# Windowed attention scored for two heads by 64 tokens and 320 keys at a time

## The chip, the cores and the metric

The kernel runs on one core of a Trainium2 chip. The core has a matrix engine (TensorE, PE in the profile; its weight loads are listed as PEld), VectorE (DVE), ScalarE (ACT), GpSimd (POOL), and SyncE (SP), which issues most of the DMA transfers. The metric is the device time of one execution in microseconds (us), and the smaller one is better.

## The reference

One encoder layer is applied to two groups of 2048 tokens of width 1024 (prompt and sample), which share their weights. Two groups of attention heads read one projection of the normalised input; their gated outputs are joined, projected and added to the input, and a gated embedding is added at the end. The change lies in head group A: 8 query heads of 64 elements, 2 key heads, each serving 4 query heads, and a window of 128 tokens to either side, with a learned sink per head in the denominator.

```python
def windowed_gqa_sink(q, k, v, sink):          # A_BLOCK = WINDOW = 128
    span = A_BLOCK + 2 * WINDOW                # 384 keys for 128 queries
    band = np.abs(si - WINDOW - qi) <= WINDOW
    def block(j):
        sc = jnp.einsum('bqkgd,bskd->bkgqs', qb, kb).astype(jnp.float32) * scale
        sc = jnp.where(valid, sc, -jnp.inf)
        m = jnp.maximum(jnp.max(sc, axis=-1, keepdims=True), sink_f)
        e = jnp.exp(sc - m)
        denom = jnp.sum(e, axis=-1, keepdims=True) + jnp.exp(sink_f - m)
        pr = (e / denom).astype(vb.dtype)
        o = jnp.einsum('bkgqs,bskd->bqkgd', pr, vb)
        return o.reshape(b, A_BLOCK, A_WIDTH)
...
o_a = windowed_gqa_sink(q_a, k_a, v_a, sink_a) * jax.nn.silu(g_a)
```

Of the 384 keys that a block of 128 queries may see, a run of 64 queries sees 320: its own 64 and 128 on either side.

## The kernel before, in words

The kernel has three stages. The first (32 blocks of 128 tokens, numbered f; 16 per sequence, t within it) projects the input for head group A and does its windowed attention. The second does the same for head group B, the neighbourhood attention. The third multiplies the joined outputs with the output and gate weights. Products are made in three parts of a number's high and low half, so that a score product has the high and low half of the keys stacked on the 128 rows of TensorE's array (`ks_a`), and a value product has the high and low half of a value side by side in its 128 columns (`vv`).

TensorE's order is written out by hand: every product (`mm`, line 259) and transpose (`tr`, line 262) is chained to the one before. The main loop draws projection products of the blocks ahead from a stream ("filler": 24 products of 256 columns named `pk`, and 48 of 512 columns named `pq` and `pg`, for each block), and between them puts the steps of attention. A block has two units, one for each key head (`unit_a`, line 652). The list `PLAN_A` (line 88) says at which fraction of a unit's share of filler each step comes; an entry with 1 is a step of this unit, one with 0 a step of the unit before. The other engines mostly follow in order of their readiness.

The steps of one unit before the change, for an interior block (three key blocks of 128):

- `sc` 0 to 3: for each of the unit's four query heads, two products of 384 columns (128 queries by 384 keys; queries' high and low parts) in a PSUM tile, then on DVE one pass that adds the mask and takes the row maximum (`softmax`, line 272). Behind the fourth, `exps` (line 282) makes the exponentials and their sums on ACT.
- `rest`: the second part of the queries' split into high and low halves, which `prep` starts for the next block (`prep_a`, line 641: four transposes `pqt`).
- `den`: the sink is added to the sums, the reciprocal taken, and the gate multiplied by it on POOL.
- `pt` 0 to 2: for each key block, four transposes (one per head) of the exponentials into one PSUM tile, copied out by ACT (high part, line 678) and subtracted by DVE (low part, line 679) into one of three `p_t` buffers.
- `po` 0 to 2: for each key block, two products of 512 columns (four heads by 128 queries) with the values, all three blocks adding up in one PSUM bank.
- `fin`: two transposes of the gate (`pgt`), the sum of high and low value columns, the gating, and the transfer to memory.

At a sequence's first and last block (t = 0 and t = 15) there are two key blocks, so 256 columns of scores, eight transposes and four value products.

Of the kernel before, what the change touches and what calls it, by code (L numbers as in the profile page):

```python
# [11 lines left out]
F32 = mybir.dt.float32  # L12
# [41 lines left out]
def bias_offsets():  # L54
# [31 lines left out]
CP = 2  # L86
KB = 23
PLAN_A = (
    (0.04, 1, "sc", 0), (0.10, 1, "sc", 1), (0.12, 1, "sc", 2), (0.12, 1, "rest", 0), (0.14, 1, "sc", 3),
    (0.14, 1, "rest", 1), (0.14, 0, "po", 0),  # L90
    (0.22, 0, "po", 1), (0.34, 0, "po", 2), (0.36, 1, "den", 0), (0.45, 0, "fin", 0), (0.46, 1, "prep", 0),
    (0.75, 1, "pt", 0), (0.79, 1, "pt", 1), (0.88, 1, "pt", 2),
)
PLAN_B = (
# [6 lines left out]
def emit(ctx, tc, io):  # L101
# [167 lines left out]
                mm(ps, xr[:, a, k, :], w(k, b), k == 0 and i == 0, k == KT - 1 and i == 2)  # L269
                yield cost, k == KT - 1 and i == 2  # L270

    def softmax(i, ps, n, bias, sm):

        s = main.tile([128, 512], F32, tag="s", name="s", bufs=SB)
        nc.vector.tensor_tensor_reduce(out=s[:, :n], in0=ps[:, :n], in1=bias, scale=1.0, scalar=-3.0e38,  # L275
                                       op0=ALU.add, op1=ALU.max, accum_out=sm["mx"][:, i:i + 1])
        sm["s"].append(s)

    def sm_tiles():
        return {"s": [], **{k: ap.tile([128, 4], F32, tag=k, name=k, bufs=3) for k in ("mx", "nm", "den", "rd")}}  # L280

    def exps(sm, n, fct, gs, sink=None):

        mx, nm, den, rd, ss = (sm[k] for k in ("mx", "nm", "den", "rd", "s"))
        if sink is None:
            nc.vector.tensor_scalar_mul(nm, mx, -1.0)  # L286
            yield
        else:
            nc.vector.scalar_tensor_tensor(out=nm, in0=mx, scalar=-1.0, in1=sink[1], op0=ALU.mult, op1=ALU.min)
        for n_, i in enumerate((0, 2, 1, 3) if sink is None else range(4)):  # L290
            ex = nc.scalar.activation(ss[i][:, :n], ss[i][:, :n], AF.Exp, bias=nm[:, i:i + 1],  # L291
                                      accum_out=den[:, i:i + 1])
            if sink is None and n_ == 0:
                P(ex)
        if sink is not None:
            es = ap.tile([128, 4], F32, tag="es", name="es", bufs=3)
            nc.vector.tensor_tensor(out=es, in0=sink[0], in1=nm, op=ALU.add)
            nc.scalar.activation(es, es, AF.Exp)
            yield
            nc.vector.tensor_tensor(out=den, in0=den, in1=es, op=ALU.add)  # L300
        nc.vector.reciprocal(out=rd, in_=den)
        nc.vector.tensor_scalar_mul(rd, rd, fct)
        g2 = ap.tile([128, 4, HD], F32, tag="g2", name="g2", bufs=2)
        nc.gpsimd.tensor_tensor(out=g2, in0=gs.rearrange("p (h d) -> p h d", h=4),
                                in1=rd.unsqueeze(2).broadcast_to([128, 4, HD]), op=ALU.mult)
        sm["g2"] = g2.rearrange("p h d -> p (h d)")
        yield
# [129 lines left out]
    sums = [dram.tile([4, 128, 4, 512], F32, tag=f"sums{i}", name=f"sums{i}") for i in range(2)]  # L437
    w_gate_c = copied(io["w_gate"], DM, 1024)
    snk = ap.tile([128, 2, 8], F32, tag="snk", name="snk")
    nc.sync.dma_start(snk[:, 0, :], io["sink"].partition_broadcast(128))  # L440
    nc.vector.tensor_scalar_mul(snk[:, 1, :], snk[:, 0, :], -1.0)
    tab = [ap.tile([128, 2, NT, 16], F32, tag="vp", name=f"tab{i}", bufs=3) for i in range(2)]
    for i in range(4):
# [3 lines left out]
        raws_g += load_first(main.tile([128, 2, 512], F32, tag="p_t", name="ws", bufs=3), j, 768, 512)  # L447
    for j in range(4, KT):
        raws_g += load_first(ap.tile([128, 1, 512], F32, tag="qg", name="wg", bufs=6), j, 768, 512)
    mask = ap.tile([128, 384], F32, tag="vp", name="mask", bufs=3)  # L450
    nc.sync.dma_start(mask, io["band"])
    load_next()
    load_next()
# [187 lines left out]
    def prep_a(f):  # L641
        q = held[f][0]
        pqt = ptile([128, 512], "ms", "pqt")
        for i in range(4):
            tr(pqt[:, 128 * i:128 * i + 128], q[:, 2 * i:2 * i + 2, :].rearrange("p h d -> p (h d)"))
        q1 = [ap.tile([128, 512], F32R, tag="q1", name="q1", bufs=3) for _ in range(2)]
        q2 = [q2s[f % 2][:, e] for e in range(2)]
        drain(split_q(pqt, q1, q2, 0))
        qrest[f] = split_q(pqt, q1, q2, 1)
        return q1, q2  # L650

    def unit_a(f, kv):
        s, t = divmod(f, NT)
        _, gs, y = held[f]
        k0, k1 = max(0, t - 1), min(NT, t + 2)
        n = 128 * (k1 - k0)
        m0 = 128 * (k0 - t + 1)
        sm, prs, got = sm_tiles(), [], {}

        def sc(i):  # L660
            ps = ptile([128, 512], "sc", "sc")
            for j, q in enumerate(qs[f]):
                mm(ps[:, :n], q[kv][:, 128 * i:128 * i + 128], ks_a[:, kv, 128 * k0:128 * k1], j == 0, j == 1)
            softmax(i, ps, n, mask[:, m0:m0 + n], sm)
            if i == 3:
                got["ex"] = exps(sm, n, y[:, 11:12], gs[:, 256 * kv:256 * kv + 256],
                                 (snk[:, 0, 4 * kv:4 * kv + 4], snk[:, 1, 4 * kv:4 * kv + 4]))
                next(got["ex"])

        def pt(j):  # L670
            if j >= k1 - k0:
                return
            pt = ptile([128, 4, 128], "pt", "pt")
            for i in range(4):
                tr(pt[:, i, :], sm["s"][i][:, 128 * j:128 * j + 128])
            pr = main.tile([128, 2, 512], F32R, tag="p_t", name="pr", bufs=3)
            pf = pt.rearrange("p h q -> p (h q)")
            nc.scalar.copy(pr[:, 0], pf)
            nc.vector.tensor_tensor(out=pr[:, 1], in0=pf, in1=pr[:, 0].bitcast(F32), op=ALU.subtract)
            prs.append(pr)  # L680

        def po(j):
            if j == 0:
                got["po"] = ptile([128, 512], "ms", "po")
            if j < k1 - k0:
                v = vv[:, k0 + j, kv].rearrange("p a d -> p (a d)")
                for i in range(2):
                    mm(got["po"], v, prs[j][:, i], j == 0 and i == 0, k0 + j == k1 - 1 and i == 1)

        def fin(_):  # L690
            pgt = ptile([128, 2, 128], "sc", "pgt")
# [3 lines left out]
            ph2 = got["po"].rearrange("p (i e q) -> p e i q", e=2, q=128)  # L695
            for e in range(2):
                a, z = 64 * e, 64 - 64 * e
                nc.scalar.copy(ot[a:a + 64], ph2[z:z + 64, e])
            for e in range(2):
                a = 64 * e  # L700
                nc.vector.tensor_tensor(out=ot[a:a + 64], in0=ph2[a:a + 64, e], in1=ot[a:a + 64], op=ALU.add)
            nc.vector.tensor_tensor(out=ot, in0=pgt, in1=ot, op=ALU.mult)
# [105 lines left out]
    def unit_b(f):  # L808
# [25 lines left out]
        def sc(h):  # L834
            ps = ptile([128, 512], "sc", "scb")
            for j, q in enumerate(qs[f]):
                mm(ps[:, :n].rearrange("p (r c) -> p r c", c=ncol), q[h % 2][:, 128 * (h // 2):128 * (h // 2) + 128],
                   ks_b[h % 2][:, r0:r0 + nr, h // 2, c0:c0 + ncol], j == 0, j == 1)
            softmax(h, ps, n, bias[:, h, :n], sm)
            if h == 3:  # L840
                got["ex"] = exps(sm, n, hr_b[:, st:st + 1], gs)
                next(got["ex"])

        def pt(x):
# [82 lines left out]
    def ple_ahead(n, tail=False):  # L927

        load_p(n + 1)
        for m in range(KT):  # L930
            ps = ptile([128, TW], "pj", "pple")
            if m == 5 and n + 1 < len(tiles):
                split_p(n + 1)
            flush("p0")
            for k in range(2):
                w, c = early["p"][2 * (m // 4) + k], 128 * (m % 4)
                for i, (a, b) in enumerate(((0, 0), (0, 1), (1, 0))):
                    mm(ps, w[:, a, c:c + 128], p_rs[n][:, k, b], k == 0 and i == 0, k == 1 and i == 2)
                    yield 215
            if tail:  # L940
                ev = main.tile([128, TW], F32, tag="s", name="ev", bufs=SB)
            else:
                ev = ap.tile([128, TW], F32, tag=("ev", "sq")[m // 2 % 2], name="ev", bufs=2)
            P(nc.scalar.copy(ev, ps))
            nc.sync.dma_start(ple_d[n][:, m], ev)

# [315 lines left out]


def _band():
    q = np.arange(128)[:, None]
    k = np.arange(384)[None, :]
    return np.where((k >= q) & (k <= q + 256), 0.0, NEG).astype(np.float32)


# [68 lines left out]
```

## Time and profile before

| what | value |
|---|---|
| median of three runs | 2495.81 us (2495.41 to 2498.2) |
| the profiled execution, its time | 2493.45 us |
| its span in the profile | 2491.5 us |
| granted TensorE clock | 1.0 |
| busy: PE, PEld, DVE, ACT, POOL | 99%, 84%, 70%, 57%, 32% |
| first stage's attention, about | 42 to 774 us of the span |

The span runs from the first to the last instruction of the profiled execution; its time also holds what lies around it. PE counts as busy while any product is in its pipeline, and successive products overlap, so that a product's listed length is longer than its share of PE; the distance between the starts of successive products is that share. A row of a group names the line of code, engine, operation, output and inputs, shapes and count, then busy time, the mean length of one in ns, and the engine's idle time before it with what ended that.

### The profile page before, as it was taken

What the parts mean: (1) busy time and instruction counts of PE and PEld (TensorE: products, weight loads), DVE (VectorE), ACT (ScalarE), POOL (GpSimd) and SP (SyncE); (2) the same over time, 40 slices, a digit from 0 to 9 for tenths busy, and PEclk for the clock granted to TensorE, in tenths of its full rate; (3) what the DMA queues carried; (4) which work ended last, traced back from release to release, by engine and by line L of the source; (5) the groups of instructions that cost most, each with busy time, mean ns of one, the idle gap of its engine ahead of it and who ended that gap; (6) DMA issues with size and microseconds to landing.
All of it is one profiled execution on the core that took longest, in us unless ns stands there. A gap on an engine that the chain in (4) does not pass through costs nothing.

```text
span 2491.5 us, 39866 instructions
## 1 busy us (share of the span) xinstructions
PE 2470.3 (99%) x12920; PEld 2084.8 (84%) x12920; DVE 1733.7 (70%) x4274; ACT 1417.0 (57%) x3341; POOL 786.7 (32%) x1033
## 2 busy tenths in 40 slices
PE   9999999999999999999999999999999999999999
PEld 7888888888888888888888888888788888888887
DVE  7777777777775666666666676776547655687776
ACT  6677766767664566665566666665664222344443
POOL 4444444444434444444444443443110000000000
PEclk9999999999999999999999999999999999999999
DMA  6432233222254466556855566666977455756765
GB/s 207 140 111 97 82 94 100 90 92 94 90 183 139 145 196 183 166 181 189 272 184 182 184 208 197 199 204 217 302 245 279 155 172 176 265 172 219 243 226 169
DMA packets 246656, 438.86 MB, mean 176 GB/s; under 512 B 31920, under 2 KB 86320, under 8 KB 241200
## 3 DMA queue, kind: packets, MB, share of 16 engines
q1 hardware_dynamic: 246160, 436.30, 54.3%
q8 instruction: 103, 1.69, 0.3%
q14 instruction: 105, 0.86, 0.1%
q10 hardware_dynamic: 288, 0.01, 0.0%
HBM read 308.28 MB, written 133.19 MB: 177 GB/s over the span
## 4 chain that ended last, share of the span: by engine, by line
PE 93%; DMA 3%; DVE 2%; ACT 1%; issue 1%; POOL 0%; SPq 0%; DVEq 0%; ACTq 0%; POOLq 0%
PE pvg L260 14%; PE pqk L260 14%; PE acca L1161 13%; PE accc L1161 10%; PE pg L260 7%; PE pq L260 7%; PE scb L260 3%; PE ptb L263 3%; PE sc L260 3%; PE po L260 3%; PE pob L260 3%; PE pk L260 3%; PE pt L263 3%; PE pple L260 3%; DMA p<-p_t 1%; DMA stn<-x_n 1%
## 5 line engine op out<-in xcount | busy, mean ns | idle before, releaser
L291 ACT ACTIVATE s<-s,nm 128x384 f32<-128x384 f32 (+4 forms) x512 | 307.2, 601 | 328.4 <-DVE nm L286 199.5
L260 PE MATMUL pvg<-wb,xr 128*128 128x512 f32 x1536 | 461.4, 407 | 0.0
L260 PE MATMUL pqk<-wa,xr 128*128 128x512 f32 x1536 | 442.3, 410 | 0.0
L260 PEld LDWEIGHTS pqk<-wa,xr 128*128 128x128 f32 x1536 | 266.3, 189 | 37.0
L260 PEld LDWEIGHTS pvg<-wb,xr 128*128 128x128 f32 x1536 | 266.9, 189 | 31.7 <-DVE wb L157 0.8
L356 POOL TENSOR_TENSOR xr<-stx,xr 128x512 fp32r<-128x512 f32 x188 | 241.5, 1294 | 162.5 <-ACT xr L355 154.8
L1143 ACT CAST opd<-raw 128x512 fp32r<-128x512 f32 x224 | 131.5, 618 | 268.4 <-PE acca L1161 115.6
L1144 DVE TENSOR_TENSOR opd<-raw,opd 128x512 fp32r<-128x512 f32 x224 | 146.5, 686 | 143.8 <-ACT opd L1143 143.8
L260 PE MATMUL pg<-wb,xr 128*128 128x512 f32 x768 | 231.5, 409 | 1.0 <-DVE vv L506 1.0
L260 PE MATMUL pq<-wa,xr 128*128 128x512 f32 x768 | 220.5, 400 | 1.4 <-DVE wa L157 1.1
L275 DVE CUSTOM_DVE_ANT_0 s<-scb,bias 128x288 f32<-128x288 f32 (+3 forms) x256 | 141.8, 555 | 103.9 <-PE scb L260 99.0
L142 POOL TENSOR_TENSOR yb<-vrb,power 128x8 f32<-128x8 f32 x64 | 105.3, 1645 | 252.5 <-DVE vrb L747 244.2
L1161 PE MATMUL accc<-opd,wb 128*128 128x512 f32 x768 | 176.7, 389 | 0.0
L1161 PE MATMUL acca<-opd,wa 128*128 128x512 f32 x768 | 175.5, 389 | 0.0
L1161 PE MATMUL acca<-opd,s 128*128 128x512 f32 x768 | 175.4, 389 | 0.0
L1161 PEld LDWEIGHTS acca<-opd,wa 128*128 128x128 f32 x768 | 144.1, 188 | 29.9
L1161 PEld LDWEIGHTS acca<-opd,s 128*128 128x128 f32 x768 | 144.2, 188 | 29.9
L1161 PEld LDWEIGHTS accc<-opd,wb 128*128 128x128 f32 x768 | 144.1, 188 | 29.9
L873 DVE TENSOR_TENSOR otb<-pob,otb 64x512 f32<-64x512 f32 x128 | 88.2, 689 | 112.8 <-ACT otb L872 111.7
L260 PEld LDWEIGHTS pq<-wa,xr 128*128 128x128 f32 x768 | 139.2, 188 | 24.8 <-DVE wa L157 1.9
L260 PEld LDWEIGHTS pg<-wb,xr 128*128 128x128 f32 x768 | 137.1, 189 | 21.9 <-DVE vv L506 1.5
L260 PEld LDWEIGHTS pob<-p_t,vw 128*128 128x128 f32 (+2 forms) x832 | 132.0, 189 | 25.3 <-DVE p_t L854 5.3
(159 smaller groups left out, 5117.8 us busy)
## 6 DMA issues: line engine op xcount, KB each, us to landing
stx<-x_b SPq DMA_DIRECT2D x128, 256.0 KB
vw<-v_d SPq DMA_DIRECT2D x112, 256.0 KB
stx<-x_a SPq DMA_DIRECT2D x64, 256.0 KB
stn<-x_n SPq DMA_DIRECT2D x64, 256.0 KB
v_d<-vb SPq DMA_DIRECT2D x64, 256.0 KB
ple_d<-ev SPq DMA_DIRECT2D x64, 256.0 KB
xres<-x_r SPq DMA_DIRECT2D x64, 256.0 KB
x_d<-r SPq DMA_DIRECT2D x64, 256.0 KB
```

What stands on the lines that cost most here:

```text
L142: nc.gpsimd.tensor_tensor(out=y, in0=v, in1=power.broadcast_to([128, n]), op=ALU.pow)
L260: pinned(nc.tensor.matmul(out, lhsT, rhs, start=start, stop=stop))
L263: pinned(nc.tensor.transpose(out, in_, eye))
L275: nc.vector.tensor_tensor_reduce(out=s[:, :n], in0=ps[:, :n], in1=bias, scale=1.0, scalar=-3.0e38, op0=ALU.add, op1=ALU.max, accum_out=sm[ ...
L291: ex = nc.scalar.activation(ss[i][:, :n], ss[i][:, :n], AF.Exp, bias=nm[:, i:i + 1], accum_out=den[:, i:i + 1])
L356: low.tensor_tensor(out=lo, in0=raw, in1=hi.bitcast(F32), op=ALU.subtract)
L873: nc.vector.tensor_tensor(out=ot[a:a + 64], in0=pq[a:a + 64], in1=ot[a:a + 64], op=ALU.add)
L1143: P(nc.scalar.copy(hi, v))
L1144: P(nc.vector.tensor_tensor(out=lo, in0=v, in1=hi.bitcast(F32), op=ALU.subtract))
L1161: pinned(nc.tensor.matmul(ps, w[k][:, a, c:c + 128], o[:, b], start=i in (0, 1, 4) and k == 0 and j == 0, stop=k == 3 and j == 2, skip_gro ...
```

## The change

The two axes "head" and "half of the queries" are exchanged. A score product now takes two heads by 64 queries instead of one head by 128 queries, so that its 128 rows share one run of 64 tokens, and covers 320 keys instead of 384. `prep_a` writes the transposed queries in that order. The scores of the two halves of a pair of heads lie side by side in one tile of 640 columns (`s2`; three buffers).

The transposes are regrouped by keys. Step `pt` 1 takes the whole key block before for the first half and the whole key block after for the second; `pt` 2 takes the middle block for both. What is left is 64 keys for each half (the lower half of the block after for the first half, the upper half of the block before for the second); these lie next to one another in the tile, and `pt` 0 transposes them together, two transposes of 128 columns, to a tile of 256 columns. In the value products (`part`) of that tile, the first half uses rows 0 to 63 with the lower half of one value block, and the second half uses rows 64 to 127 with the upper half of another. The product on the upper rows is put in the third `po` step and is made to wait for the last score reduction of the next unit, which is behind the product on the lower rows.

The sink has to be added with heads and halves exchanged back, which takes four small additions instead of one; the sink's values are spread by two small copies at the start. At a sequence's end a piece of the score tile is cleared by POOL. In the plan, `po` 0 moves ahead of the fourth scores, `po` 1 from 0.22 to 0.26, `po` 2 from 0.34 to 0.37.

```diff
 PLAN_A = (
-    (0.04, 1, "sc", 0), (0.10, 1, "sc", 1), (0.12, 1, "sc", 2), (0.12, 1, "rest", 0), (0.14, 1, "sc", 3),
-    (0.14, 1, "rest", 1), (0.14, 0, "po", 0),
-    (0.22, 0, "po", 1), (0.34, 0, "po", 2), (0.36, 1, "den", 0), (0.45, 0, "fin", 0), (0.46, 1, "prep", 0),
+    (0.04, 1, "sc", 0), (0.10, 1, "sc", 1), (0.12, 1, "sc", 2), (0.12, 1, "rest", 0), (0.14, 0, "po", 0), (0.14, 1, "sc", 3),
+    (0.14, 1, "rest", 1),
+    (0.26, 0, "po", 1), (0.36, 1, "den", 0), (0.37, 0, "po", 2), (0.45, 0, "fin", 0), (0.46, 1, "prep", 0),
...
     def exps(sm, fct, gs, sink=None):
...
-            nc.vector.tensor_tensor(out=den, in0=den, in1=es, op=ALU.add)
+            for half in range(2):
+                for e in range(2):
+                    rows = slice(64 * e, 64 * e + 64)
+                    nc.vector.tensor_tensor(out=rd[64 * half:64 * half + 64, e::2], in0=den[rows, half::2],
+                                            in1=es[rows, half::2], op=ALU.add)
+            den = rd
...
+    for e in range(2):
+        rows = slice(64 * e, 64 * e + 64)
+        nc.vector.tensor_copy(snk[rows, 0].rearrange("p (a b) -> p a b", b=2),
+                              snk_all[rows, e::2].unsqueeze(2).broadcast_to([64, 4, 2]))
...
-    mask = ap.tile([128, 384], F32, tag="vp", name="mask", bufs=3)
+    mask = ap.tile([128, 320], F32, tag="vp", name="mask", bufs=3)
...
+        halves = pqt.rearrange("p (r x e q) -> p r e x q", r=2, x=2, e=2)
         for i in range(4):
-            tr(pqt[:, 128 * i:128 * i + 128], q[:, 2 * i:2 * i + 2, :].rearrange("p h d -> p (h d)"))
+            tr(halves[:, i // 2, i % 2], q[:, 2 * i:2 * i + 2, :].rearrange("p h d -> p (h d)"),
+               ident.rearrange("p (x q) -> p x q", x=2))
...
+        left, right = t > 0, t < NT - 1
+        span = [(0 if left else 128 - 64 * half, 320 if right else 256 - 64 * half) for half in range(2)]
...
         def sc(i):
+            pair, half = divmod(i, 2)
+            a, z = span[half]
+            c0, n = 128 * t - 128 + 64 * half, z - a
+            if half == 0:
+                pairs.append(ap.tile([128, 640], F32, tag="ev", name="s2", bufs=3))
+                if not right:
+                    nc.gpsimd.memset(pairs[pair][:, 256:320], 0.0)
             ps = ptile([128, 512], "sc", "sc")
             for j, q in enumerate(qs[f]):
-                mm(ps[:, :n], q[kv][:, 128 * i:128 * i + 128], ks_a[:, kv, 128 * k0:128 * k1], j == 0, j == 1)
-            softmax(i, ps, n, mask[:, m0:m0 + n], sm)
+                mm(ps[:, :n], q[kv][:, 128 * i:128 * i + 128], ks_a[:, kv, c0 + a:c0 + z], j == 0, j == 1)
+            seen[:] = softmax(i, ps, n, mask[:, a:z], sm, pairs[pair][:, 320 * half + a:320 * half + z]), i
...
         def pt(j):
-            pt = ptile([128, 4, 128], "pt", "pt")
-            for i in range(4):
-                tr(pt[:, i, :], sm["s"][i][:, 128 * j:128 * j + 128])
+            pt = ptile([128, 512], "pt", "pt")
+            r, c = slice(0, 128), slice(0, 512)
+            if j == 0:
+                r, c = slice(0 if right else 64, 128 if left else 64), slice(0, 256)
+                for pair in range(2):
+                    tr(pt[:r.stop, 128 * pair:128 * pair + 128], pairs[pair][:, 256:256 + r.stop])
+            else:
+                if j == 1:
+                    c = slice(0 if left else 256, 512 if right else 256)
+                for x in range(c.start // 128, c.stop // 128):
+                    half, pair = divmod(x, 2)
+                    col = ((0, 512), (128, 384))[j - 1][half]
+                    tr(pt[:, 128 * x:128 * x + 128], pairs[pair][:, col:col + 128])
...
+        def part(j, d, rows, cols, at, first=False, last=False, behind_max=False):
+            for i in range(2):
+                mm(got["po"][:, at:at + cols.stop - cols.start], vv[rows, t + d, kv].rearrange("p a d -> p (a d)"),
+                   prs[j][rows, i, cols], first and i == 0, last and i == 1)
+                if behind_max and i == 0:
+                    tc.add_manual_dep(last_pe[-1], seen[0].ins.name,
+                                      mybir.DependencyInfo(mybir.DependencyClass.Sync, mybir.DependencyReason.DATA),
+                                      reason="lower rows' products done")
+
         def po(j):
+            full, low, high = slice(0, 128), slice(0, 64), slice(64, 128)
+            first, second = slice(0, 256), slice(256, 512)
             if j == 0:
                 got["po"] = ptile([128, 512], "ms", "po")
-            if j < k1 - k0:
-                v = vv[:, k0 + j, kv].rearrange("p a d -> p (a d)")
-                for i in range(2):
-                    mm(got["po"], v, prs[j][:, i], j == 0 and i == 0, k0 + j == k1 - 1 and i == 1)
+                if right:
+                    part(0, 1, low, first, 0, True)
+                    part(1, 1, full, second, 256)
+                else:
+                    part(0, -1, high, first, 256, True)
+                if left:
+                    part(1, -1, full, first, 0)
+                got["order"] = seen[1:]
+            elif j == 1:
+                part(2, 0, full, slice(0, 512), 0, False, not (left and right))
+            elif left and right:
+                assert seen[1] == 3 and got["order"] == [2]
+                part(0, -1, high, first, 256, False, True, True)
```

More of the change, by code (lines that the diff above doesn't have):

```diff
@@ L270, in project, with softmax, exps @@
                 yield cost, k == KT - 1 and i == 2
[L272 to L276, printed above, removed]
+    def softmax(i, ps, n, bias, sm, s=None):
+        if s is None:
+            s = main.tile([128, 512], F32, tag="s", name="s", bufs=SB)[:, :n]
+        highest = nc.vector.tensor_tensor_reduce(out=s, in0=ps[:, :n], in1=bias, scale=1.0, scalar=-3.0e38,
+                                                 op0=ALU.add, op1=ALU.max, accum_out=sm["mx"][:, i:i + 1])
         sm["s"].append(s)
+        return highest
     def sm_tiles():
         return {"s": [], **{k: ap.tile([128, 4], F32, tag=k, name=k, bufs=3) for k in ("mx", "nm", "den", "rd")}}
-    def exps(sm, n, fct, gs, sink=None):
+    def exps(sm, fct, gs, sink=None):
         mx, nm, den, rd, ss = (sm[k] for k in ("mx", "nm", "den", "rd", "s"))
@@ L290, in exps @@
         for n_, i in enumerate((0, 2, 1, 3) if sink is None else range(4)):
-            ex = nc.scalar.activation(ss[i][:, :n], ss[i][:, :n], AF.Exp, bias=nm[:, i:i + 1],
-                                      accum_out=den[:, i:i + 1])
+            ex = nc.scalar.activation(ss[i], ss[i], AF.Exp, bias=nm[:, i:i + 1], accum_out=den[:, i:i + 1])
             if sink is None and n_ == 0:
@@ L439, in emit @@
     snk = ap.tile([128, 2, 8], F32, tag="snk", name="snk")
-    nc.sync.dma_start(snk[:, 0, :], io["sink"].partition_broadcast(128))
+    snk_all = ap.tile([128, 8], F32, tag="snk_all", name="snk_all")
+    nc.sync.dma_start(snk_all, io["sink"].partition_broadcast(128))
+    for e in range(2):
+        rows = slice(64 * e, 64 * e + 64)
+        nc.vector.tensor_copy(snk[rows, 0].rearrange("p (a b) -> p a b", b=2),
+                              snk_all[rows, e::2].unsqueeze(2).broadcast_to([64, 4, 2]))
     nc.vector.tensor_scalar_mul(snk[:, 1, :], snk[:, 0, :], -1.0)
@@ L650, in prep_a @@
         return q1, q2
+    seen = []
     def unit_a(f, kv):
@@ L654, in unit_a @@
         _, gs, y = held[f]
[L655 to L658, printed above, removed]
+        left, right = t > 0, t < NT - 1
+        span = [(0 if left else 128 - 64 * half, 320 if right else 256 - 64 * half) for half in range(2)]
+        sm, pairs, prs, got = sm_tiles(), [], [], {}
         def sc(i):
+            pair, half = divmod(i, 2)
[5 more added lines that the diff above has]
+                    nc.gpsimd.memset(pairs[pair][:, 256:320], 0.0)
             ps = ptile([128, 512], "sc", "sc")
             for j, q in enumerate(qs[f]):
-                mm(ps[:, :n], q[kv][:, 128 * i:128 * i + 128], ks_a[:, kv, 128 * k0:128 * k1], j == 0, j == 1)
-            softmax(i, ps, n, mask[:, m0:m0 + n], sm)
+                mm(ps[:, :n], q[kv][:, 128 * i:128 * i + 128], ks_a[:, kv, c0 + a:c0 + z], j == 0, j == 1)
+            seen[:] = softmax(i, ps, n, mask[:, a:z], sm, pairs[pair][:, 320 * half + a:320 * half + z]), i
             if i == 3:
-                got["ex"] = exps(sm, n, y[:, 11:12], gs[:, 256 * kv:256 * kv + 256],
+                got["ex"] = exps(sm, y[:, 11:12], gs[:, 256 * kv:256 * kv + 256],
                                  (snk[:, 0, 4 * kv:4 * kv + 4], snk[:, 1, 4 * kv:4 * kv + 4]))
@@ L670, in pt @@
         def pt(j):
-            if j >= k1 - k0:
-                return
-            pt = ptile([128, 4, 128], "pt", "pt")
-            for i in range(4):
-                tr(pt[:, i, :], sm["s"][i][:, 128 * j:128 * j + 128])
+            pt = ptile([128, 512], "pt", "pt")
[11 more added lines that the diff above has]
+                    tr(pt[:, 128 * x:128 * x + 128], pairs[pair][:, col:col + 128])
@@ L676, in pt @@
             pr = main.tile([128, 2, 512], F32R, tag="p_t", name="pr", bufs=3)
-            pf = pt.rearrange("p h q -> p (h q)")
-            nc.scalar.copy(pr[:, 0], pf)
-            nc.vector.tensor_tensor(out=pr[:, 1], in0=pf, in1=pr[:, 0].bitcast(F32), op=ALU.subtract)
+            nc.scalar.copy(pr[r, 0, c], pt[r, c])
+            nc.vector.tensor_tensor(out=pr[r, 1, c], in0=pt[r, c], in1=pr[r, 0, c].bitcast(F32), op=ALU.subtract)
             prs.append(pr)
+        def part(j, d, rows, cols, at, first=False, last=False, behind_max=False):
[6 more added lines that the diff above has]
+                                      reason="lower rows' products done")
@@ L694, in fin @@
             ot = ap.tile([128, 2, 128], F32, tag="ot", name="ot", bufs=2)
-            ph2 = got["po"].rearrange("p (i e q) -> p e i q", e=2, q=128)
+            ph2 = got["po"].rearrange("p (x i e q) -> p e x i q", x=2, i=2, e=2)
+            oh = ot.rearrange("p i (x q) -> p x i q", x=2)
             for e in range(2):
                 a, z = 64 * e, 64 - 64 * e
-                nc.scalar.copy(ot[a:a + 64], ph2[z:z + 64, e])
+                nc.scalar.copy(oh[a:a + 64], ph2[z:z + 64, e])
             for e in range(2):
                 a = 64 * e
-                nc.vector.tensor_tensor(out=ot[a:a + 64], in0=ph2[a:a + 64, e], in1=ot[a:a + 64], op=ALU.add)
+                nc.vector.tensor_tensor(out=oh[a:a + 64], in0=ph2[a:a + 64, e], in1=oh[a:a + 64], op=ALU.add)
             nc.vector.tensor_tensor(out=ot, in0=pgt, in1=ot, op=ALU.mult)
@@ L840, in sc @@
             if h == 3:
-                got["ex"] = exps(sm, n, hr_b[:, st:st + 1], gs)
+                got["ex"] = exps(sm, hr_b[:, st:st + 1], gs)
                 next(got["ex"])
@@ L942, in ple_ahead @@
             else:
-                ev = ap.tile([128, TW], F32, tag=("ev", "sq")[m // 2 % 2], name="ev", bufs=2)
+                ev = ap.tile([128, TW], F32, tag=("ev", "sq")[m // 2 % 2], name="ev", bufs=3 - m // 2 % 2)
             P(nc.scalar.copy(ev, ps))
@@ L1264, in _band @@
 def _band():
-    q = np.arange(128)[:, None]
-    k = np.arange(384)[None, :]
+    q = np.arange(128)[:, None] % 64
+    k = np.arange(320)[None, :]
     return np.where((k >= q) & (k <= q + 256), 0.0, NEG).astype(np.float32)
```

## The prediction

> **What bounds the kernel now.** I read the page first: the span, the busy shares, and the chain of waits.
>
> ```profile
> span 2491.5 us, 39866 instructions
> PE 2470.3 (99%) x12920; PEld 2084.8 (84%) x12920; DVE 1733.7 (70%) x4274; ACT 1417.0 (57%) x3341; POOL 786.7 (32%) x1033
> PEclk9999999999999999999999999999999999999999
> PE 93%; DMA 3%; DVE 2%; ACT 1%; issue 1%; POOL 0%; SPq 0%; DVEq 0%; ACTq 0%; POOLq 0%
> ```
>
> TensorE (PE) is busy for 99% at an unthrottled clock, and 93% of the chain that ended last runs on it. As an average may hide a stage with another limit, I next took the windows by stage. The second row, 42 to 774 us, is the first stage, where the change lies; columns are the length, then busy time and instructions of PE, weight loads, VectorE (DVE), ScalarE (ACT), GpSimd (POOL), and the clock.
>
> ```profile
> 0.00:42.00 42.00, 37.57 (x184) 30.25 (x185) 29.35 (x70) 28.02 (x57) 17.14 (x36) 1.00 0.67 235
> 42.00:774.00 732.00, 728.51 (x4161) 634.31 (x4160) 568.28 (x1703) 506.00 (x1350) 330.68 (x531) 1.00 0.34 108
> ```
>
> PE is idle for 3.5 us of 732, while DVE has 22% free and ACT 31%. But busy PE overlaps its own products, so what counts is the distance from one start to the next. I read those from PE's timeline of one interior token block. Columns: start, length of the merged row, engine, line, operation, tiles, shape, count.
>
> ```profile
> 450.50 0.51 PE L260 MATMUL sc<-ks_a,q 128*128 128x384 f32 x2
> 450.85 0.63 PE L260 MATMUL pq<-wa,xr 128*128 128x512 f32 x2
> 451.32 0.86 PE L260 MATMUL sc<-ks_a,q 128*128 128x384 f32 x4
> 452.02 0.40 PE L260 MATMUL pq<-wa,xr 128*128 128x512 f32 x1
> 452.25 0.51 PE L260 MATMUL sc<-ks_a,q 128*128 128x384 f32 x2
> 452.60 0.63 PE L260 MATMUL po<-pr,vv 128*128 128x512 f32 x2
> 453.06 0.62 PE L260 MATMUL pq<-wa,xr 128*128 128x512 f32 x2
> 454.91 0.61 PE L260 MATMUL po<-pr,vv 128*128 128x512 f32 x2
> 458.36 0.60 PE L263 MATMUL pt<-ident,s 128*128 128x128 f32 x4
> 458.72 0.48 PE L260 MATMUL pq<-wa,xr 128*128 128x512 f32 x1
> 459.03 0.60 PE L263 MATMUL pt<-ident,s 128*128 128x128 f32 x4
> 467.39 0.38 PE L263 MATMUL pgt<-ident,g 128*128 128x128 f32 x2
> 467.53 0.48 PE L260 MATMUL pg<-wb,xr 128*128 128x512 f32 x1
> 467.85 0.60 PE L263 MATMUL pqt<-ident,q 128*128 128x128 f32 x4
> 468.99 1.34 PE L260 MATMUL pk<-wx,xr 128*128 128x256 f32 x10
> 470.16 0.60 PE L263 MATMUL pt<-ident,s 128*128 128x128 f32 x4
> 473.61 0.51 PE L260 MATMUL sc<-ks_a,q 128*128 128x384 f32 x2
> ```
>
> A product of 512 columns takes (453.06 - 452.60)/2 = 0.23 us, one of 384 columns (452.02 - 451.32)/4 = 0.175, one of 256 (470.16 - 468.99)/10 = 0.117. Four transposes and a 512-column product take 459.03 - 458.36 = 0.67, so the four cost 0.44; two cost 467.85 - 467.39 - 0.23 = 0.23.
>
> As a test I add up a whole block: 48 x 0.23 + 24 x 0.117 of projections; twice (8 x 0.175 + 3 x 0.44 + 6 x 0.23 + 0.23) of attention; 0.55 for five transposes of queries and keys. That is 13.85 + 8.66 + 0.55 = 23.06 us, and the trace has 473.61 - 450.50 = 23.11. The stage is the sum of PE's starts. Every PE nanosecond saved or added counts in full, as long as no other engine makes PE stand.
>
> **The change, part by part.** There are 64 units (2 sequences x 16 blocks x 2 key heads): 56 interior and 8 at a sequence's ends.
>
> *Scores.* An interior unit keeps its 8 score products, each of 320 columns instead of 384. From 256 to 384 columns the price rises by 0.058 us, 0.45 ns a column; 64 columns fewer are 0.029 us. The second stage shows that the slope goes on between those widths:
>
> ```profile
> 1205.40 0.33 PE L260 MATMUL scb<-ks_b,q1b 128*128 128x360 f32 x1
> 1205.56 0.32 PE L260 MATMUL scb<-ks_b,q 128*128 128x360 f32 x1
> 1207.51 0.47 PE L260 MATMUL pob<-p_t,vw 120*128 120x256 f32 x3
> 1207.82 0.43 PE L260 MATMUL pqk<-wa,xr 128*128 128x512 f32 x1
> 1208.09 0.33 PE L260 MATMUL scb<-ks_b,q1b 128*128 128x360 f32 x1
> ```
>
> 360 columns take 1205.56 - 1205.40 = 0.16 (by the slope 0.164). So: 8 x 0.029 = 0.232 us saved.
>
> *Transposes.* 12 become 10, as the half blocks of both halves go together: one group of four becomes a group of two, 0.44 - 0.23 = 0.21 us saved.
>
> *Products with the values.* Six of 512 columns become two of 512 and eight of 256: 8 x 0.117 + 2 x 0.23 - 6 x 0.23 = 0.016 us added. No column is saved: four of the eight use 64 of 128 rows, and a product is paid by columns.
>
> Sum: 0.232 + 0.21 - 0.016 = 0.426 us per interior unit, 56 x 0.426 = 23.9 us. The end units keep 8 transposes and as many value columns; half of their score products go from 256 to 192 columns. That is worth between nothing and 8 x 4 x 0.029 = 0.9 us; I take nothing, since transposes at 0.11 us show that narrow operations stop getting cheaper.
>
> *Half-row products.* This is the unknown. Nothing in the trace multiplies on 64 rows. Each interior unit has one pair on the lower rows (in the first "po" step) and one on the upper rows (in the third), so PE goes from all rows to half and back twice: 4 changes; an end unit has 2, and the four units at a sequence's start also transpose 64 columns, 2 more. That makes 224 + 16 + 8 = 248 changes at a price s. For the low end the nearest rows are the three 120-row products above: 1208.09 - 1207.51 = 0.58 = 3 x 0.117 + 0.23, so going to fewer rows and back costs nothing; nor does going between transposes and products, beyond the 0.01 that a small group shows (0.23 for two against 0.22). For the high end:
>
> ```profile
> L260 PEld LDWEIGHTS po<-pr,vv x368: 186/188/195, 52.6 to 772.4; 128*128 128x128 f32 x184
> L260 PE MATMUL po<-pr,vv x368: 389/393/507, 52.7 to 772.4; 128*128 128x512 f32 x184
> ```
>
> A product lasts 0.39 us while the next starts after 0.23, so 0.16 us of its end lie under the next one, and a weight load lasts 0.188 us under the one before. If a change of rows forbade the first overlap, s = 0.16; the second, s = 0.188; both, 0.35. A gain below nothing is excluded: both products of a pair use the same rows, and their neighbours use all. I take 0.01, for the nearest rows, all of which change the use of the array without a visible price: 2.5 us. Break-even is 23.9/248 = 0.096 us.
>
> The Trainium skill speaks against this choice: "TensorEngine Tiling (Array Packing)", section "Tiling Modes", Key Properties, says that changing the tiling mode, not just the tile, drains TensorE, and counts 64 rows by 128 columns as a mode of its own. It gives no price, and no run here shows it yet; it is the first rival below.
>
> *VectorE and ScalarE*, rows of the first stage by form:
>
> ```profile
> L679 DVE TENSOR_TENSOR pr<-pt,pr 128x512 fp32r<-128x512 f32 x184 | 123.1, 682 | 23.4 <-ACT pr L678 23.0
> L275 DVE CUSTOM_DVE_ANT_0 s<-sc,mask 128x384 f32<-128x384 f32 x224 | 117.6, 553 | 8.1 <-PE sc L260 6.1
> L275 DVE CUSTOM_DVE_ANT_0 s<-sc,mask 128x256 f32<-128x256 f32 x32 | 12.5, 420 | 1.6 <-PE sc L260 1.3
> L702 DVE TENSOR_TENSOR ot<-pgt,ot 128x256 f32<-128x256 f32 x63 | 26.4, 419 | 1.1
> L300 DVE TENSOR_TENSOR den<-den,es 128x4 f32<-128x4 f32 x64 | 11.0, 172 | 98.9 <-ACT es L298 98.9
> ```
>
> Per interior unit on DVE: four score reductions lose 64 columns at (553 - 420)/128 = 1.04 ns, -0.27 us; one of three low-part subtractions goes to half width, 682 to about 419, -0.26; the sink's addition becomes four, 3 x 0.172 = +0.52. That is level, and its cover is DVE's 22% of free time. ACT loses columns only. Costed at nothing.
>
> *Order and buffers.* The first value step moves ahead of the fourth scores and has six products, not two; the second goes from 0.22 to 0.26 of a unit's 11.55 us, the third from 0.34 to 0.37, +0.35 us. Outputs are read at 0.45 as before. The first transposed buffer is now held to 0.37 of the next unit; three serve, and the fourth is asked for at 0.75, 4.4 us later. Two score pairs per unit rotate through three buffers: the second pair, needed at 0.12 of the next unit, comes free after the transposes at 0.88, 2.8 us earlier. The upper pair newly waits on PE for the fourth score reduction; behind it stand the projections, so any lateness is PE's in full:
>
> ```profile
> 453.25 0.56 DVE L275 CUSTOM_DVE_ANT_0 s<-sc,mask 128x384 f32<-128x384 f32 x1
> ```
>
> That reduction ends at 453.81 and the third step stands at 454.91, in the new order near 455.2; moved behind four more products (0.47 us) but shortened, the reduction still leaves about a microsecond. Nothing charged. Eight memsets on POOL (55% idle in this stage) write columns that no reduction reads. At the start, two small DVE copies join the queue behind the sink's transfer, whose size stays; by the 0.172 us of the small addition they are worth 0 to 0.35 us once. The mask's transfer shrinks and no other is added.
>
> **Sum.** -23.9 + 2.5 = -21.4 us. The profiled execution took 2493.45 us, 1.95 outside its span; -21.4 gives 2472.0. The median of the runs shown, 2495.81, lies 2.4 above that execution, so I forecast 2474. The three runs spread over 2.8 us, so about 0.2% (5 us) is what a measurement can tell from no change.
>
> **The rivals.**
>
> 1. *Draining at each change of rows (slower).* Place: before and after each half-row pair. Price 0.16 us a change, the hidden end of a product: 248 x 0.16 = 39.7, net +15.8, 2512 us; with 0.188, +22.7, 2518; with both, +62, 2558. It decides from s = 0.096 on. For it: the change makes TensorE use a part of the array that the trace never shows. Against: 120-row products and transposes change for free. By the skill's rule named above this is what happens, if the drain is as long as a product's end.
>
> 2. *A short drain near the break-even,* s between 0.076 and 0.117: within 5 us of no change, about 2496.
>
> 3. *Narrower scores gain nothing,* if weight loads (PEld busy 634 of 732 us) set the pace: then only the transposes are saved, 56 x 0.194 = 10.9 us, less 2.5: 2487. Against it: the 360-column rows follow the slope, and the 256-column ones are at 0.117.
>
> 4. *The new wait bites.* The fourth reduction would have to be about 1.4 us later than above before it eats the gain (one microsecond of slack and 0.43 of gain); one more microsecond costs 56 us. DVE runs its reductions back to back here, and all PE idle in this stage is 3.5 us.
>
> **Chances.** Forecast (s under 0.076): 0.47, own range 2468 to 2491. Rival 3: 0.03. Rival 2: 0.06. Rival 1: 0.32 to 2518, and 0.08 above. Rival 4: 0.04. So faster 0.50, same 0.06, slower 0.44. The range reaches from 2467 (s = 0, the end units' 0.9 us and the runs' spread) to 2518 (s = 0.188) and leaves out about 0.15.
>
> **What would show it.** Right: score products near 0.146 us apart, ten transposes, interior block near 22.3 us, and the first 512-column product behind a half-row pair starting 0.23 us after the pair's second. Wrong: gaps around "po" pairs of 64 rows of 0.1 us and more, without a releaser; or a row in which PE waits for DVE at the upper pair.

## The result and the profile after

The changed kernel takes 2519.45 us (median of four runs, 2518.69 to 2522.69) against 2495.78 us before: a ratio of 1.0096, 95% interval 1.0084 to 1.0109. It is 24 us slower, where 22 us less were forecast, and lies just above the range.

The page of the changed kernel, first lines and the head of the chain:

```profile
span 2517.2 us, 40298 instructions
PE 2496.5 (99%) x13048; PEld 2076.9 (83%) x13048; DVE 1729.7 (69%) x4476; ACT 1391.6 (55%) x3349; POOL 791.0 (31%) x1041
PE 93%; DMA 2%; DVE 2%; ACT 1%; issue 1%; POOL 0%; SPq 0%; DVEq 0%; ACTq 0%; POOLq 0%
```

PE is as full as before and carries the same share of the chain. The page alone would not say why 128 more products cost 26 us of span. PE's timeline does. One interior block runs from one group of query transposes to the next (... marks rows left out):

```profile
461.43 0.60 PE L263 MATMUL pqt<-ident,q 128*128 128x128 f32 x4
...
467.76 0.74 PE L260 MATMUL sc<-ks_a,q 128*128 128x320 f32 x4
468.34 0.40 PE L260 MATMUL pq<-wa,xr 128*128 128x512 f32 x1
468.67 1.17 PE L260 MATMUL po<-pr,vv 64*128 64x256 f32 x6
469.68 0.46 PE L260 MATMUL sc<-ks_a,q 128*128 128x320 f32 x2
...
470.67 0.62 PE L260 MATMUL po<-pr,vv 128*128 128x512 f32 x2
471.13 1.08 PE L260 MATMUL pq<-wa,xr 128*128 128x512 f32 x4
472.14 0.50 PE L260 MATMUL po<-pr,vv 64*128 64x256 f32 x2
472.57 0.73 PE L260 MATMUL pq<-wa,xr 128*128 128x512 f32 x2
473.13 0.38 PE L263 MATMUL pgt<-ident,g 128*128 128x128 f32 x2
...
485.33 0.60 PE L263 MATMUL pqt<-ident,q 128*128 128x128 f32 x4
```

The block takes 485.33 - 461.43 = 23.90 us (23.88 in most others) instead of 23.11. The scores are as cheap as forecast: (468.34 - 467.76)/4 = 0.145 us each. The time is lost around the half-row pairs, the two products on the lower 64 rows (`low`) and the two on the upper ones (`high`). From 471.13 to 473.13 stand six products of 512 columns and the two of the upper pair, which by the prices of before are 6 x 0.23 + 2 x 0.117 = 1.61 us, and took 2.00: 0.39 too much. From 468.34 to 469.68 (one of 512, six of 256, where the row "x6" starts with the lower pair) it is 1.34 instead of 0.93: 0.41 too much.

The weight loads in the same place show what is lost (same columns):

```profile
470.44 0.42 PEld L260 LDWEIGHTS po<-pr,vv 128*128 128x128 f32 x2
470.90 0.88 PEld L260 LDWEIGHTS pq<-wa,xr 128*128 128x128 f32 x4
472.14 0.29 PEld L260 LDWEIGHTS po<-pr,vv 64*128 64x128 f32 x2 [0.35 <-DVE vr L532]
472.57 0.30 PEld L260 LDWEIGHTS pq<-wa,xr 128*128 128x128 f32 x2
...
483.88 0.29 PEld L260 LDWEIGHTS po<-pr,vv 64*128 64x128 f32 x2 [0.35 <-issue]
```

Normally a load starts 0.23 us ahead of its product (470.44 against 470.67) and lies under the product before. At the half-row pair, and again behind it, load and product start at the same time: 472.14 and 472.14, 472.57 and 472.57. Four products from 471.13 on would let the next start at 472.05; the load begins 0.09 later. The pair then takes 472.57 - 472.14 = 0.43 instead of 0.234, and the two products behind it 473.13 - 472.57 = 0.56 instead of 0.46. So at each change about 0.09 us pass before the load begins, and then about 0.11 us of the load are uncovered: 0.20 us, four times in an interior unit's pass, twice per pair. How the pair's 0.43 divides is not visible in these merged rows; the rows of the two adjacent pairs further down show it. The releaser in the brackets is an inference of the profile, and no cause: DVE's operation ends at 472.04, a tenth of a microsecond earlier, but the same pair of the next unit, at 483.88, stands for the same 0.35 us and waits for nothing that the profile shows ("issue").

With 56 x 4 + 8 x 2 = 240 changes between all rows and half the rows, 240 x 0.2 = 48 us, less the 23.9 us that were saved, gives +24.1 us; +23.7 were measured. That the two are so close is partly luck: the price and the saving are those of the regular interior blocks, and in the whole kernel both come out smaller, as the first experiment shows.

### The profile page after: what moved, and what is told of

It is laid out like the page before. It is cut to its first block, busy times and chain, and to the rows that moved or that the text cites. A ratio compares the mean times of both kernels' runs of the same rounds, so it can differ in the third digit from the quotient of the medians.

```text
span 2517.2 us, 40298 instructions
## 1 busy us (share of the span) xinstructions
PE 2496.5 (99%) x13048; PEld 2076.9 (83%) x13048; DVE 1729.7 (69%) x4476; ACT 1391.6 (55%) x3349; POOL 791.0 (31%) x1041
## 4 chain that ended last, share of the span: by engine, by line
PE 93%; DMA 2%; DVE 2%; ACT 1%; issue 1%; POOL 0%; SPq 0%; DVEq 0%; ACTq 0%; POOLq 0%
PE pqk L260 14%; PE pvg L260 14%; PE acca L1210 13%; PE accc L1210 10%; PE pq L260 7%; PE pg L260 7%; PE po L260 5%; PE scb L260 3%; PE ptb L263 3%; PE pob L260 3%; PE pk L260 3%; PE sc L260 3%; PE pple L260 3%; PE pt L263 3%; DMA stn<-x_n 1%
## 5 line engine op out<-in xcount | busy, mean ns | idle before, releaser
L293 ACT ACTIVATE s<-s,nm 128x320 f32<-128x320 f32 (+6 forms) x512 | 294.3, 576 | 342.9 <-DVE nm L288 196.0
```

Source lines behind the costliest of these rows:

```text
L293: ex = nc.scalar.activation(ss[i], ss[i], AF.Exp, bias=nm[:, i:i + 1], accum_out=den[:, i:i + 1])
```

## The experiments

Theory A is this price of a change of rows. Theory B is a price per half-row product. Theory C blames the rest of the edit: the new wait, the order, the small additions. All ratios are to the kernel before, run beside them on the same chip.

**All rows instead of half, all else kept.** POOL copies the half value blocks into a tile whose other half is zero, once per block; the pairs multiply 128 rows by it.

```diff
+            nc.gpsimd.tensor_copy(vz[f % 2][rows, half], vv[rows, t + d].rearrange("p k a d -> p k (a d)"))
...
-                mm(got["po"][...], vv[rows, t + d, kv].rearrange("p a d -> p (a d)"),
-                   prs[j][rows, i, cols], first and i == 0, last and i == 1)
+                w = vz[f % 2][:, rows.start // 64, kv] if j == 0 else vv[:, t + d, kv].rearrange("p a d -> p (a d)")
+                mm(got["po"][...], w, prs[j][:, i, cols], first and i == 0, last and i == 1)
```

> The changed kernel with its order, its wait and its product counts, but no product on 64 rows: the values are copied by POOL into a tile with zeros in the other half, so that the pairs multiply all 128 rows, and the end units transpose 128 columns. Theory A (248 changes between all and half rows cost 0.19 us each, 47.6 us): 2519.5 - 47.6 = 2472 us. Theory B (a half-row product is itself slow, about 0.19 us more for each of 240 products): the same 2472. Theory C (the new wait, the new order or the small additions cost the time): it stays near 2519.

Measured: 2475.22 us, ratio 0.9923 (0.9910 to 0.9935). PE's timeline of an interior block:

```profile
458.27 0.60 PE L263 MATMUL pqt<-ident,q 128*128 128x128 f32 x4
...
465.18 0.40 PE L260 MATMUL pq<-wa,xr 128*128 128x512 f32 x1
465.41 0.40 PE L260 MATMUL po<-pr,vz 128*128 128x256 f32 x2
465.65 0.64 PE L260 MATMUL po<-pr,vv 128*128 128x256 f32 x4
466.12 0.45 PE L260 MATMUL sc<-ks_a,q 128*128 128x320 f32 x2
...
480.54 0.60 PE L263 MATMUL pqt<-ident,q 128*128 128x128 f32 x4
```

The stretch that took 1.34 us takes 466.12 - 465.18 = 0.94, and the block 22.27 us; the prediction's sum without any price for the half rows was 23.11 - 2 x 0.426 = 22.26. Theory C falls: order, wait and small additions are the same here.

Over the whole kernel the gain is 19.3 us, not 23.9. The regular interior blocks gain what was forecast, but others do not. From the second to the third group of query transposes of each sequence it is 22.35 and 22.34 us, where the kernel before takes 22.25 and 22.26; sixteen narrower scores and two transposes fewer should save 0.65 of that. PE loses the time in small pieces around the transposes there, and why is open. The two blocks with the wait told of below take 47.48 us together; the kernel before takes 48.15 there, so that 48.15 - 4 x 0.426 = 46.45 were due. These places make up 2.5 of the 4.6 us; the rest is not settled. Against the changed kernel the difference of the ratios is 43 us, or 0.18 us for each of the 240 changes, a little under the 0.20 of the regular blocks.

**Each half-row pair twice in a row,** so that the result counts those keys twice.

```diff
-            for i in range(2):
+            half = rows.stop - rows.start == 64
+            for n, i in enumerate((0, 1, 0, 1) if half else (0, 1)):
```

> The changed kernel with each half-row pair done twice in a row (four products instead of two; the output is off by that). Theory A (price per change of rows): 120 pairs x 2 x 0.117 us more, +28, about 2547 us. Theory B (price per half-row product, 0.117 + 0.19 each): 120 x 2 x 0.31 = +74, about 2593. Theory C: +28 at most.

Measured: 2544.07 us, ratio 1.0199 (1.0185 to 1.0213). Against the changed kernel's 1.0096 that is about 26 us for 240 more half-row products, 0.11 us each, near the 0.117 that a product of 256 columns costs on all rows. Theory B falls. On the timeline the longer upper pair takes 470.09 - 469.42 = 0.67 us against 0.43:

```profile
469.42 0.73 PE L260 MATMUL po<-pr,vv 64*128 64x256 f32 x4
470.09 0.73 PE L260 MATMUL pg<-wb,xr 128*128 128x512 f32 x2
```

**The lower pair taken apart by a product on all rows,** with no product more.

```diff
-                    part(0, 1, low, first, 0, True)
-                    part(1, 1, full, second, 256)
+                    for i in range(2):
+                        part(0, 1, low, first, 0, True, which=(i,))
+                        part(1, 1, full, second, 256, which=(i,))
```

> The changed kernel with the lower pair of 60 units taken apart: a product on all rows, which was behind the pair, stands between its two products. The products are the same in number. Theory A: two more changes in 60 units, 120 x 0.19 = +23, about 2542 us. Theory B and theory C: nothing, about 2519.

Measured: 2542.38 us, ratio 1.0189 (1.0175 to 1.0203), about 23 us over the changed kernel for 120 more changes, 0.19 us each, by nothing but the order of the same products. That is theory A.

**The price alone, in the kernel before.** The middle key block's two products use part of the rows, or part of the columns, in the 56 interior units. What they leave out (half or three quarters of that block's keys, or the low halves of its values) is missing from the result.

```diff
-                    mm(got["po"], v, prs[j][:, i], j == 0 ...
+                    r = slice(0, 64 if j == 1 and k1 - k0 == 3 else 128)     # 32 in the second kernel
+                    mm(got["po"], v[r], prs[j][r, i], j == 0 ...
```

```diff
+                    c = slice(0, 64 if j == 1 and k1 - k0 == 3 else 128)     # the third kernel
+                    mm(got["po"][c], v[:, c], prs[j][:, i], j == 0 ...
```

> The kernel before, with the two value products of the middle key block on rows 0 to 63 alone in the 56 interior units (half of that block's keys are left out). Nothing else changes. Theory A: 112 changes x 0.19 = +21.5, about 2517 us. Theory B: 112 products x 0.19, the same. Theory C: no change, 2496. If the price hangs on the length of the half-row product (512 columns here, 256 in the change), it comes out as another price per change than 0.19.

> As e4_before_64_rows (the kernel before, middle value products on part of the rows), but on 32 rows: three quarters of that block's keys are left out. Theory A: the price is that of a change, whatever the part: 112 x 0.197 = +22 us over the kernel before. Rival: the price grows or shrinks with the number of rows in use, so it differs from +22.

> The kernel before, with the two value products of the middle key block of the 56 interior units on all rows, but with 64 of the 128 value columns (their low halves are left out). If the price hangs on the part of the array that is in use, as theory A has it, narrower columns are a change too: 112 x 0.197 = +22 us over the kernel before. If it hangs on rows alone: 0 (the products stream as many columns as before).

Measured: with 64 rows 2516.63 us, ratio 1.0087 (1.0072 to 1.0103); with 32 rows 2516.48 us, 1.0085 (1.0071 to 1.0099); with 64 columns 2496.63 us, 1.0005 (0.9996 to 1.0014). So 22.1 and 21.3 us for 112 changes, 0.20 and 0.19 us each, whether 64 or 32 rows are left, and, beside the changed kernel, whether the product has 512 or 256 columns; and nothing that can be measured for half the columns. The timelines, first of 64 rows:

```profile
463.33 0.62 PE L260 MATMUL pq<-wa,xr 128*128 128x512 f32 x2
463.88 0.73 PE L260 MATMUL po<-pr,vv 64*128 64x512 f32 x2
464.54 1.20 PE L260 MATMUL pq<-wa,xr 128*128 128x512 f32 x4
465.58 0.62 PE L260 MATMUL po<-pr,vv 128*128 128x512 f32 x2
```

and of 64 columns:

```profile
463.46 0.62 PE L260 MATMUL pg<-wb,xr 128*128 128x512 f32 x2
463.92 0.61 PE L260 MATMUL po<-pr,vv 128*64 128x512 f32 x2
464.37 1.09 PE L260 MATMUL pg<-wb,xr 128*128 128x512 f32 x4
465.30 0.62 PE L260 MATMUL po<-pr,vv 128*128 128x512 f32 x2
```

Eight products of 512 columns take 465.58 - 463.33 = 2.25 us with the half rows in the middle and 465.30 - 463.46 = 1.84 with the half columns (8 x 0.23).

The Trainium skill, "TensorEngine Tiling (Array Packing)", section "Tiling Modes", says that changing the mode drains TensorE; for rows this case agrees, at 0.2 us. The same section counts 128 rows by 64 columns as a mode too, and there the measurement differs: 112 such changes cost 1.5 us together by the medians, and no more than 3.5 us, 0.03 each, by an interval that holds zero as well. The row shows that 64 columns are in use; whether the array was in the mode of that name, no run here shows.

**Both pairs next to each other,** lower then upper, in the third step of the interior units; the upper one writes to a bank of its own.

```diff
-                part(0, -1, high, first, 256, False, True, True)
+                part(0, 1, low, first, 0, False, True)
+                part(0, -1, high, first, 256, True, True, bank=ptile([128, 512], "sc", "px"))
```

> The changed kernel with the lower pair of the 56 interior units moved to directly before the upper pair, in the third step; the upper pair writes to a bank of its own that nobody reads (its part of the result is left out). Theory A with a price for going between all and half rows alone: two changes fewer per unit, 112 x 0.2 = -22, about 2497 us against 2519. If going from the lower to the upper rows costs as much: -11, about 2508. If the lower and the upper pair run side by side, up to 56 x 0.234 = 13 us less than the first: about 2484.

Measured: 2484.47 us, ratio 0.9956 (0.9941 to 0.9971), 34 us under the changed kernel: the third of the expectations, 22 us for the changes spared and 13 us because the pairs run at the same time. The timeline shows the second directly:

```profile
473.22 1.08 PE L260 MATMUL pq<-wa,xr 128*128 128x512 f32 x4
474.23 0.38 PE L260 MATMUL po<-pr,vv 64*128 64x256 f32 x1
474.23 0.38 PE L260 MATMUL px<-pr,vv 64*128 64x256 f32 x1
474.45 0.28 PE L260 MATMUL po<-pr,vv 64*128 64x256 f32 x1
474.46 0.28 PE L260 MATMUL px<-pr,vv 64*128 64x256 f32 x1
474.66 0.50 PE L260 MATMUL pq<-wa,xr 128*128 128x512 f32 x1
```

Four half-row products take 474.66 - 474.23 = 0.43 us, as much as the two of a single pair did, and going from the lower rows to the upper costs no visible time. The rows also divide the price of the changes: the second product starts 474.45 - 474.23 = 0.22 us after the first, 0.10 more than its 0.117, and the first on all rows 474.66 - 474.45 = 0.21 after the second, 0.09 more. Both pairs in one bank were not tried. The time of this kernel lacks the addition of the second bank, so it isn't a version to use as it stands.

**The padded kernel without the new wait,** once with both pairs in the first step, once in the same order (whose edit is shown).

```diff
-                part(0, -1, high, first, 256, False, True, True)
+                part(0, -1, high, first, 256, False, True)
```

> The kernel with padded values on all rows (e1_full_rows), with both pairs in the first value step and no wait on the score reduction. In e1_full_rows that wait made PE stand once for 2.05 us. Theory: about 2 us under e1_full_rows, a ratio of about 0.9915 to the kernel before; rival: the six products in one place delay the fourth scores and with them the exponentials, and it is level.

> The kernel with padded values on all rows (e1_full_rows) in the same order, but without the upper pair's wait on the fourth score reduction, which all rows no longer need. If the wait itself costs what its one row in e1_full_rows shows (2.05 us): about 0.1% better than e1_full_rows, a ratio to the kernel before near 0.9915. If the lateness of DVE at that place stops PE anyhow at the next step, as the kernel with both pairs in the first step suggests: level with e1_full_rows, 0.992 to 0.993.

Measured: 2480.12 us, ratio 0.9937 (0.9925 to 0.9950), and 2477.44 us, 0.9925 (0.9911 to 0.9938). Neither is better than 0.9923. The wait shows in the changed kernel, and longer in the padded one, each time once, near the end of the first sequence. Among the waits of PE in the changed kernel:

```profile
PE po L260 <- DVE mx L276: 1.4, 1, 1.4
```

Without it, in the same order, PE stands at other steps of the same blocks instead; these are rows of that kernel's timeline in which PE was idle:

```profile
349.27 0.63 PE L263 MATMUL pqt<-ident,q 128*128 128x128 f32 x4 [0.66 <-DVE ks_a L497]
352.23 0.33 PE L263 MATMUL pt<-ident,s 128*128 128x128 f32 x1 [0.35 <-ACT s L293]
355.48 0.66 PE L263 MATMUL pt<-ident,s 128*128 128x128 f32 x4 [1.53 <-DVE ot L768]
```

The two blocks from one group of query transposes to the next but one take 47.69 us without the wait and 47.48 with it. The releasers are inferred, but most of them are DVE: it is late in those blocks in any case, and the wait was one of several places where that reaches PE.

The padded kernel is the best version here that computes the whole layer, and no better without the wait: 0.77% under the kernel before, where the change was 0.96% above it.

## Why the prediction was wrong

*What bounds the kernel: right for the regular blocks.* There a PE start saved or added counts in full: 22.26 us forecast and 22.27 found without half rows, and with four pairs 22.27 + 8 x 0.20 = 23.87 against 23.90. At the sequences' starts and in a few blocks it does not, so that the padded kernel shows 19.3 us of the 23.9.

*Scores, transposes and value products: right.* 0.145 us per score product was found for 0.146, and products of 256 columns cost the same on half the rows (0.11 us by the doubled pairs). The saving of 0.426 us per unit is confirmed by the padded kernel's block. Rival 3, that narrower scores gain nothing, falls with it.

*Other engines at nothing: right for their work.* Between the first and the last group of query transposes, the same 31 blocks' work, DVE is busy for 545.5 us, against 550.0 before; it is the third busy time in these rows, the first of the kernel before, the second of the changed one.

```profile
36.88:747.92 711.04, 708.24 (x4061) 618.55 (x4061) 549.97 (x1652) 491.85 (x1311) 321.61 (x523) 1.00 0.34 108
38.60:773.98 735.38, 731.77 (x4183) 607.12 (x4182) 545.46 (x1840) 466.56 (x1319) 326.16 (x528) 1.00 0.33 105
```

The small copies at the start were put at 0 to 0.35 us. The first scores start at 43.8 us instead of 42.1, but that is no measure of the copies: the start lies anywhere between 41.6 and 44.1 us in the runs, at 43.9 in the kernel before with 32 rows, whose start was not touched. What PE loses around the transposes at a sequence's start may belong under this head; it was not settled.

*Half-row products: this step failed.* "I take 0.01, for the nearest rows, all of which change the use of the array without a visible price" was the wrong choice between the low end and the high end. Products on 120 rows, transposes, and, as the runs added, products on 64 columns cost nothing extra, but they were not near: none of them leaves half the rows out. (The second stage of the kernel before also multiplies on 96 rows: three products of 256 columns and four of 512 take 837.69 - 836.40 = 1.29 us, by the prices 1.27. Between 64 and 96 rows nothing was measured.) The price was 0.20 us, above the break-even of 0.096 that the prediction had worked out, so rival 1 came true with its place and its sign. Its size was between the bounds and matched none: neither the hidden end of a product alone (0.16) nor a load alone (0.188) nor both lengths together (0.35), but 0.09 us until the load may begin and 0.11 us of the load. The listed lengths of product and load hold time that overlaps even here, so that the bounds should have been distances between starts. Of the 248 changes, 8 were transposes with fewer columns and all rows; the value products with fewer columns were free, and these 8 were not measured by themselves.

*Rival 4: right in kind and small.* The new wait bit once, for 1.4 us (2.05 in the padded kernel), and taking it away from the padded kernel gained nothing that could be measured.

## What to carry to other kernels

Before a product is put on 64 or 32 rows, count how often the stream of products goes from all rows to fewer and back: at 0.20 us each, that is nearly the time of a whole 512-column product, and here the four changes of a unit cost 0.8 us where the rest of the change saved 0.43. Padding the weights with zeros cost nothing in TensorE's time here (0.94 us for a stretch that the prices put at 0.93), since a product is paid by its columns; where rows must be split, put the halves of several pairs together, in different banks, so that two changes serve them all and the lower and upper rows run at the same time. And where the trace shows no case of an operation, ask whether the rows taken as nearest share the feature in doubt; here none did, and the first rival, which named it, was worth more than three free neighbours that didn't.

## What was not expected of the hardware

- Weight loads at a change of rows start with their product instead of 0.23 us ahead of it, and 0.09 us after the last product's turn is over, on the way in and on the way out.
- The price is the same for 64 and 32 rows (0.20 and 0.19 us) and for products of 512 and 256 columns, and none can be measured for 64 of 128 columns (1.5 us for 112 changes, within the interval of nothing).
- Lower and upper rows, writing to different banks, run side by side with nothing in the kernel but their order that asks for it: four products in 0.43 us, started in pairs within 0.01 us.
